# Attention scores over 96 rows, another opening, other norm chains and end, expert gates in pieces of 16 tokens and the fourth activation quarter in SBUF

## The chip, the cores and the metric

One core of a Trainium2 chip runs the whole program. Its engines are named as in the profile: PE (TensorE's matmuls; PEld its weight loads), DVE (VectorE), ACT (ScalarE), POOL (GpSimd), SP (SyncE, which here only issues DMAs). Times are microseconds on the device. The metric is the time of one execution; the kernel before took 1413.62 us, the median of three runs (1412.87 to 1416.95).

## The reference

256 tokens of 1024 channels, float32 throughout, go through two transformer blocks.

- First block: an RMS norm; projections; causal latent attention with 8 heads, whose queries and keys have 64 plain and 32 rotated channels (a score is a product over 96); causal differential attention with 4 heads of 2 x 64 channels; sigmoid gates on both branches; the output projection `wo` and residual; then norm, a gated FFN of 2816 hidden channels and residual; a final norm.
- Second block: modulation of the norms by `c` through `ada_w`; multiscale pooling and neighbourhood attention with context; `wo2` and residual; then, for each token, product-key top-k: 8 heads choose 16 of 128 x 128 = 16384 experts each. The output is `sum of gate * gelu(h . u_e) * v_e` over the chosen experts, plus residual and a last norm.

## The kernel before, in words

**Number format.** Nearly every matmul is done as three float32r products: `x_hi*w_hi`, `x_lo*w_hi`, `x_hi*w_lo` (`mm3`, lines 171 to 173). The weights come from DRAM in pieces of 128 x 2048 (`raw`, 1 MB, three buffers, issued on SP, line 154). For each block of 1024 columns ACT rounds them to `whi` (line 133) and DVE subtracts to `wlo` (line 130, `split`), into three buffers each. So PE has a steady stream as long as SP, ACT and DVE keep up; all three work through their own queue in order, PE too.

**Who sets the order.** The Tile framework plans the order of each engine's queue when the kernel is built, by a simulated timeline: what is ready by its estimate goes first, with the order of the program as priority, so that work of a later stage fills gaps of an earlier one. `tc.issue_after(ins)` keeps instructions on the same engine behind `ins`, and `tc.high_priority()` lifts some. `feed(n)` hands out the steps of a generator of side work (`side`) at n per pair of expert blocks.

**Stages, in order.**

1. *Opening.* SP loads `x` (transposed, 8 blocks of 128 channels) in two halves of 512 KB, the second between the first two weight pieces of 512 KB each (line 155). ACT and DVE split `x` into `xh` and `xl` (lines 343, 344). POOL squares `x` in two instructions (line 359), DVE adds the halves, PE sums over channels, and `rsqrt_cols` gives the norm: one DVE instruction for each column (line 216) and a power on POOL (line 219). Three small casts (lines 409 to 413) follow the first projection in the program.
2. *First attention.* Plain query channels are kept as `qn` (two heads to 128 rows), rotated ones as `qp` (four heads to 128 rows), and keys as `kn` and `kp`. `soft` (line 494) makes the scores of two heads: for each, a product over 64 rows and one over 32 rows into the same PSUM bank (line 501, full float32, two PE records each), and the mask (line 502). The value projection of the second attention (`lin_nat`, lines 202 to 204) and the gate projection need no scores and are planned between them.
3. *`wo`, FFN.* `put_x1` (line 611) adds the residual two blocks at a time and hands the squares to `SumSq`; `scaled_split` then makes the FFN's input `hs`. The FFN's first matmuls go ahead without the norm, which `hooks` bring in later. DVE also reduces `ada_w` here (`jk`, line 316).
4. *Second block up to the top-k queries.* Its norm after `wo2` (`ss3`, `put_x3`, line 816) is computed between the first matmuls of `wq` (line 840).
5. *Up pass.* `u_pass` runs four quarters of 32 expert blocks. A pair of blocks is 48 matmuls into one bank and a Gelu on ACT (line 1049). Quarters 0 and 1 stay in SBUF (`ga`), 2 and 3 go to DRAM through a ring (line 1051). The side work beside it is 44 steps of top-k and 33 steps of gates: for 8 tokens DVE makes one-hot tables, PE multiplies them, and ACT writes the dense gates of 128 x 128 experts to DRAM (`gg_d`, line 1015). It is fed at 1.2 steps a pair up to block 60, and at 1.7 from there; 8 steps were fed before.
6. *Second pass.* `v_pass` loads the gates of 16 expert blocks for all tokens (`gh`, 2 MB, line 1071, two buffers), multiplies them with the activations (line 1078), splits, and PE accumulates into four banks over all 128 expert blocks (line 1091). Quarters 2 and 3 come back from DRAM (`gr`, line 1076). The last two blocks are ordered by output bank, so that one bank after the other is done.
7. *End.* For both token halves: modulation, residual, square, norm and output (lines 1131 to 1141).

Of the kernel before, what the change touches and what calls it, by code (L numbers as in the profile page):

```python
# [20 lines left out]
P = 128  # L21
# [42 lines left out]
def block_kernel(ctx: ExitStack, tc: tile.TileContext, a: dict, out: bass.AP, dbg=None):  # L64
# [74 lines left out]
    class Weights:  # L139
# [68 lines left out]
    def rsqrt_cols(vs, scale, nm="n", eps=None):  # L208

        n = len(vs)  # L210
        y = small.tile([P, n], F32, tag=f"{nm}y{n}", name="ny")
        t = small.tile([P, n], F32, tag=f"{nm}t{n}", name="nt")
        for i, v in enumerate(vs):
            c = slice(i, i + 1)
            if eps is None:
                nc.vector.tensor_scalar(t[:, c], v, scale, EPS, op0=OP.mult, op1=OP.add)
            else:
                nc.vector.scalar_tensor_tensor(t[:, c], v, scale, eps, op0=OP.mult, op1=OP.add)
# [3 lines left out]
    class SumSq:  # L222
# [3 lines left out]
        def __init__(self, K, ps_fn, tail=2, held=False):  # L226
            self.held = [] if held else None
            self.K, self.k, self.ps, self.head = K, 0, [ps_fn() for _ in range(2)], K - tail
            self.first = True
# [3 lines left out]
        def add(self, src, scale=None, sq=None):  # L233
# [11 lines left out]
            if k >= self.head - 1:  # L245
                if self.held is None:
                    self.total(sq, k)
                else:
                    self.held.append((sq, k))

        def total(self, sq, k):
# [3 lines left out]
            self.first = False  # L255

        def done(self):
            for h in self.held or ():
                self.total(*h)
            return [p_[:, 0:1] for p_ in self.ps]  # L260
# [89 lines left out]
    subg = b1a.tile([P, 1], F32, name="subg")  # L350
    nc.scalar.activation(subg, col("sub"), AF.Copy, scale=1.0 - LAMBDA_INIT)
# [919 lines left out]
```

## Time and profile before

| | |
|---|---|
| median of three runs | 1413.62 us |
| the profiled execution's own time | 1420.62 us |
| its span, first to last instruction | 1418.8 us |
| mean granted clock of PE | 0.984 |
| chain that ended last, by engine | PE 88%, DVE 5%, DMA 4% |
| moved by DMA | 308.86 MB, mean 218 GB/s |

The profile is of one execution. The windows give, for a stretch, the busy time of each engine with the number of instructions (x), then the mean granted share of PE's clock (1.00 is 2.4 GHz, 0.50 is 1.2 GHz), the share of time in which the DMA engines were busy, and the rate. Matmuls are pipelined: the duration of one is longer than the step from one to the next, and a busy PE is not a PE at its peak. So PE is judged by how many matmuls it gets through in a stretch.

### The profile page before, as it was taken

How to read it: one execution, taken by the hardware profiler on the slowest of the kernel's cores; microseconds unless marked ns; L12 is line 12 of the kernel's file. 1: busy time of each engine (PE TensorE's matmuls, PEld its weight loads, DVE VectorE, ACT ScalarE, POOL GpSimd, SP SyncE). 2: the span in 40 equal slices, each digit the busy share in tenths (PEclk: the TensorE clock that was granted, in tenths of full speed). 3: DMA queues.
4: the chain of work that ended last, by engine and by line, in shares of the span. 5: the costliest groups of instructions: out<-in, count | busy, mean ns of one | idle time of the engine just before them, and what ended most of it. 6: DMA issues, size and time to landing. Idle time of an engine off the chain costs nothing.

```text
span 1418.8 us, 24208 instructions
## 1 busy us (share of the span) xinstructions
PE 1375.2 (97%) x9776; PEld 1270.8 (90%) x9776; DVE 1013.1 (71%) x1749; ACT 704.9 (50%) x1030; POOL 23.8 (2%) x25
## 2 busy tenths in 40 slices
PE   7999999999999999899999999998999999999997
PEld 6967998999999888899999999998888888888885
DVE  6774777998888646699984489876536555566775
ACT  4443654454546555545454456554344454444443
POOL 1000000000000001000000000000000000000000
PEclk9998999999999999999999999999899999999999
DMA  6452456777795632444555578889975555588762
GB/s 239 154 196 82 141 169 234 269 279 267 262 328 191 218 125 72 152 170 158 187 198 180 178 257 311 296 296 321 340 287 197 190 197 199 198 300 289 262 233 86
DMA packets 88448, 308.86 MB, mean 218 GB/s; under 512 B 6416, under 2 KB 39824, under 8 KB 61200
## 3 DMA queue, kind: packets, MB, share of 16 engines
q1 hardware_dynamic: 78544, 279.26, 57.0%
q10 hardware_dynamic: 9792, 28.05, 5.0%
q8 instruction: 76, 1.25, 0.3%
q14 instruction: 36, 0.29, 0.1%
HBM read 281.08 MB, written 26.21 MB: 217 GB/s over the span
## 4 chain that ended last, share of the span: by engine, by line
PE 88%; DVE 5%; DMA 4%; issue 1%; ACT 1%; POOL 0%; SPq 0%; ACTq 0%; POOLq 0%; DVEq 0%
PE acc L1091 24%; PE psa L173 9%; PE psa L171 9%; PE psa L172 9%; PE psc L173 8%; PE psc L171 8%; PE psc L172 8%; DMA aw<-in_ada 2%; PE psb L501 2%; DVE wlo L130 2%; PE psd L1012 1%; PE psb L1012 1%; DMA gh<-ggd 1%; PE psd L771 1%; PE psb L759 1%
## 5 line engine op out<-in xcount | busy, mean ns | idle before, releaser
L133 ACT ACTIVATE whi<-raw 128x1024 fp32r<-128x1024 f32 (+1 forms) x426 | 448.0, 1053 | 502.7 <-PE psa L172 181.6
L130 DVE TENSOR_TENSOR wlo<-raw,whi 128x1024 fp32r<-128x1024 f32 (+1 forms) x426 | 517.4, 1217 | 240.6 <-ACT whi L133 236.9
L171 PE MATMUL psc<-h2h,whi 128*128 128x256 f32 x1024 | 294.3, 288 | 6.4 <-ACT whi L133 6.4
L173 PE MATMUL psc<-h2h,wlo 128*128 128x256 f32 x1024 | 293.8, 288 | 4.2 <-DVE wlo L130 4.2
L172 PE MATMUL psc<-h2l,whi 128*128 128x256 f32 x1024 | 292.7, 286 | 0.0
L171 PEld LDWEIGHTS psc<-h2h,whi 128*128 128x128 f32 x1024 | 199.8, 195 | 7.0 <-ACT whi L133 7.0
L173 PEld LDWEIGHTS psc<-h2h,wlo 128*128 128x128 f32 x1024 | 199.5, 195 | 4.9 <-DVE wlo L130 4.9
L172 PEld LDWEIGHTS psc<-h2l,whi 128*128 128x128 f32 x1024 | 199.8, 195 | 0.0
L1091 PE MATMUL acc<-wlo,wgh 128*128 128x512 f32 x512 | 160.2, 393 | 0.0
L1091 PE MATMUL acc<-whi,wgl 128*128 128x512 f32 x512 | 158.7, 390 | 0.0
L1091 PE MATMUL acc<-whi,wgh 128*128 128x512 f32 x512 | 138.5, 389 | 0.0
L1091 PEld LDWEIGHTS acc<-whi,wgl 128*128 128x128 f32 x512 | 96.1, 188 | 20.2
L1091 PEld LDWEIGHTS acc<-whi,wgh 128*128 128x128 f32 x512 | 96.0, 188 | 20.1
L1091 PEld LDWEIGHTS acc<-wlo,wgh 128*128 128x128 f32 x512 | 94.6, 188 | 19.7
L171 PE MATMUL psa<-acth,whi 128*128 128x256 f32 x352 | 99.9, 284 | 2.0 <-DVE ft L638 1.2
L173 PE MATMUL psa<-acth,wlo 128*128 128x256 f32 x352 | 99.9, 284 | 1.9 <-DVE wlo L130 1.9
L172 PE MATMUL psa<-actl,whi 128*128 128x256 f32 x352 | 99.8, 284 | 0.2 <-DVE actl L293 0.2
L171 PE MATMUL psa<-xh,whi 128*128 128x256 f32 x240 | 71.1, 296 | 8.0 <-ACT whi L133 8.0
L173 PE MATMUL psa<-xh,wlo 128*128 128x256 f32 x240 | 70.4, 293 | 2.6 <-DVE wlo L130 2.6
L172 PE MATMUL psa<-xl,whi 128*128 128x256 f32 x240 | 71.0, 296 | 0.0
L316 DVE SCALAR_TENSOR_TENSOR jk<-aw,row_c 128x1024 bf16<-128x1024 f32 x48 | 58.6, 1220 | 14.8 <-DMA aw<-in_ada 14.4
L171 PEld LDWEIGHTS psa<-acth,whi 128*128 128x128 f32 x352 | 66.9, 190 | 2.6 <-ACT whi L133 1.4
(415 smaller groups left out, 2462.6 us busy)
## 6 DMA issues: line engine op xcount, KB each, us to landing
raw<-in_uT SPq DMA_DIRECT2D x64, 1024.0 KB, 4.9
raw<-in_v SPq DMA_DIRECT2D x64, 1024.0 KB, 4.9
aw<-in_ada SPq DMA_DIRECT2D x48, 512.0 KB, 5.8
raw<-in_wgu SPq DMA_DIRECT2D x22, 1024.0 KB, 4.9
ggd<-gs ACTq DMA_DIRECT2D x32, 512.0 KB, 4.5
gh<-ggd SPq DMA_DIRECT2D x8, 2048.0 KB, 14.3
raw<-in_wA SPq DMA_DIRECT2D x14, 1024.0 KB, 5.0
raw<-in_wdn SPq DMA_DIRECT2D x11, 1024.0 KB, 7.2
```

What stands on the lines that cost most here:

```text
L130: e.tensor_tensor(dst, src, hi.bitcast(F32), op=OP.subtract)
L133: nc.scalar.activation(dst_h, src, AF.Copy)
L171: nc.tensor.matmul(ps, wh, xs[0][:, k], start=(k == 0), stop=False)
L172: nc.tensor.matmul(ps, wh, xs[1][:, k], start=False, stop=False)
L173: last_mm[0] = nc.tensor.matmul(ps, wl, xs[0][:, k], start=False, stop=(k == K - 1))
L316: nc.vector.scalar_tensor_tensor(jk, aw, 1.0, c_, op0=OP.mult, op1=OP.mult, accum_out=dst[:, t:t + 1])
L501: nc.tensor.matmul(s[:, i], q_[:, qb * P:(qb + 1) * P], k_[:, :n], start=(j == 0), stop=False)
L759: nc.tensor.matmul(s, q2[x_][hd, hp, qs_], kall[y_][hd, hp], start=(i == 0), stop=(i == 2))
L771: nc.tensor.matmul(o[:, h * 64:(h + 1) * 64], pts[:, kb * P:(kb + 1) * P], v2[:, kb, h * 64:(h + 1) * 64], start=(kb == 0), stop=(kb == 3))
L1012: nc.tensor.matmul(ps[:, t4 * P:(t4 + 1) * P], o1[:, 2 * g4 + t4 // 2, :, t4 % 2], og[:, c, 2 * g4 + t4 // 2, :, t4 % 2], start=(c == 1), ...
L1091: r = nc.tensor.matmul(acc[tt][n], x_, w_[:, n * 512:(n + 1) * 512], start=st, stop=sp)
```

## The change

- Opening: `x` comes in four quarters issued on ACT's queue ahead of all else there; the first weights in pieces of 512, 512 and 1024 columns; ACT squares `x` instead of POOL; the casts move behind the last `put_in` of the first projection.
- Norm chains: `rsqrt_cols` takes all columns in one instruction; `SumSq` keeps one PSUM bank and runs its matmuls together when asked. `put_x1` and `put_x3` work block by block and make the next stage's split at once. `mdt` gets a pool of its own.
- Attention: queries and keys of a head stand as 96 rows in `qh` and `kh`, so that a score is one product. `nope` writes the two halves of a bank into two heads, the rope's last sum is written for four heads apart, and ACT copies `kp` into all eight heads.
- Experts: gates are stored in pieces of 16 tokens and read for 8 expert blocks (1 MB), issued behind the last weight load before them in the program. Quarter 3 stays in SBUF, in memory that the side work leaves; only quarter 2 goes to DRAM. The feed is 1.6 up to block 44, then 1.5; the ring has 3 buffers.
- End: the last three blocks are ordered by bank; the first token half is scaled on ACT; the second half's last bank skips one product.

```diff
-                    for o in range(0, w, 1024 if self.fine and c == 0 else w):
-                        e = o + (1024 if self.fine and c == 0 else w)
+                    ends = (0, 512, 1024, w) if self.fine and c == 0 else (0, w)
+                    for o, e in zip(ends, ends[1:]):
                         last_load[0] = nc.sync.dma_start(self.raw[:, o:e], self.src[:, c + o:c + e])
-                        if self.fine and c + o == 0:
-                            load_x(1)
...
-        for i, v in enumerate(vs):
-            c = slice(i, i + 1)
-            if eps is None:
-                nc.vector.tensor_scalar(t[:, c], v, scale, EPS, op0=OP.mult, op1=OP.add)
...
+        if eps is None:
+            nc.vector.tensor_scalar(t, v, scale, EPS, op0=OP.mult, op1=OP.add)
...
+        def done(self):
             for tt in range(2):
-                nc.tensor.matmul(self.ps[tt][:, 0:1], sq[:, tt * P:(tt + 1) * P], ones[:, 0:1],
-                                 start=self.first, stop=(k == self.K - 1))
...
+                for i, sq in enumerate(self.sqs):
+                    nc.tensor.matmul(self.ps[:, tt:tt + 1], sq[:, tt * P:(tt + 1) * P], ones[:, 0:1],
+                                     start=(i == 0), stop=(i == len(self.sqs) - 1))
+            return self.ps[:, 0:2]
...
-        k = slice(4 * i, 4 * i + 4)
-        nc.sync.dma_start(xT[:, k], a["xT"].rearrange("p (k t) -> p k t", k=KD)[:, k])
+        k = slice(2 * i, 2 * i + 2)
+        nc.scalar.dma_start(xT[:, k], a["xT"].rearrange("p (k t) -> p k t", k=KD)[:, k])
...
-        nc.gpsimd.tensor_tensor(sq0[:, k], xT[:, k], xT[:, k], op=OP.mult)
+        nc.scalar.activation(sq0[:, k], xT[:, k], AF.Square)
...
+                for r, o in outs(j, m):
+                    nc.vector.tensor_tensor(o, x_[r, j:j + m], t1[r, :m], op=OP.add)
...
+    nc.scalar.activation(kh[64:96], kp[64:96].to_broadcast([32, 8, S]), AF.Copy)
+
+    def nope(dst, j, n, ps, rb):
+        for e in range(2):
+            r = slice(64 * e, 64 * e + 64)
+            nc.vector.tensor_tensor(dst[0:64].rearrange("p (j e) t -> p e j t", e=2)[:, e, j:j + n], ps[r],
+                                    rb[r][:, None, :].to_broadcast([64, n, S]), op=OP.mult)
...
-            ptss = soft([[(qn[b0:b0 + 64, h // 2], kn[b0:b0 + 64, h // 2]),
-                          (qp[r0:r0 + 32, h // 4], kp[r0:r0 + 32, 0])] for h in pair], qb,
-                        [z[:, h:h + 1] for h in pair])
+            ptss = soft([[(qh[:, h], kh[:, h])] for h in pair], qb, [z[:, h:h + 1] for h in pair])
...
     def put_x1(j, n, ps):
-        nc.vector.tensor_tensor(x1[:, j:j + n], ps, xT[:, j:j + n], op=OP.add)
-        for i in range(n):
-            ss1.add(x1[:, j + i])
-
-    lin_t(a["wo"], 8, KD, (mh, ml), put_x1)
+        nc.vector.tensor_tensor(x1[:, j], ps[:, 0], xT[:, j], op=OP.add)
+        nc.scalar.activation(hs[0][:, j], x1[:, j], AF.Copy, scale=col("ffn", j))
+        nc.vector.scalar_tensor_tensor(hs[1][:, j], x1[:, j], col("ffn", j), hs[0][:, j].bitcast(F32),
+                                       op0=OP.mult, op1=OP.subtract)
+        ss1.add(x1[:, j])
+
+    lin_t(a["wo"], 8, KD, (mh, ml), put_x1, grp=1)
...
-    TG = 8
+    TG, TD = 8, 16
...
-                nc.scalar.dma_start(gg_d[:, i_], gs.rearrange("p j t -> p (j t)"))
+                if h + TG == TD:
+                    nc.scalar.dma_start(gg_d[:, i_ * TG // TD], gs.rearrange("p j t -> p (j t)"))
...
-            g = ga[q][:, j:j + 2] if q < 2 else ring.tile([P, 2, S], F32, tag="gr", name="gr")
+            g = ga[q][:, j:j + 2] if q != 2 else ring.tile([P, 2, S], F32, tag="gr", name="gr")
...
-            feed(1.2 if q * QJ + j < 60 else 1.7)
+            feed(1.6 if q * QJ + j < 44 else 1.5)
...
+    ga += [None, hot.tile([P, QJ, S], F32, bufs=1, name="ga3")]
+    u_pass(3)
...
-    HJ = 16
+    HJ = 8
...
-                gh = hot.tile([P, NG, HJ, TG], F32, tag="gh", name="gh")
-                nc.sync.dma_start(gh, gg_d.rearrange("p g (j t) -> p g j t", t=TG)[:, :, jj:jj + HJ])
+                gh = hot.tile([P, S // TD, HJ, TD], F32, tag="gh", name="gh")
+                with tc.issue_after(last_load[0].ins):
+                    nc.sync.dma_start(gh, gg_d.rearrange("p g (j t) -> p g j t", t=TD)[:, :, jj:jj + HJ])
...
-                        for i in range(2):
-                            r = block(i, tt, (n,))
+                        for b in range(NE - 3, NE):
+                            r = block(b, tt, (n,))
...
-            nc.vector.tensor_tensor(xn[:, h_], o[:, h_], fg[:, h_], op=OP.mult)
+            if tt == 0 or n == 0:
+                nc.vector.tensor_tensor(xn[:, h_], o[:, h_], fg[:, h_], op=OP.mult)
...
-        nc.vector.tensor_scalar(xn[:, hs_[1]], xn[:, hs_[1]], y, None, op0=OP.mult)
+        if tt == 0:
+            nc.scalar.activation(xn[:, hs_[1]], xn[:, hs_[1]], AF.Copy, scale=y)
+        else:
+            nc.vector.scalar_tensor_tensor(xn[:, hs_[1]], o[:, hs_[1]], y, fg[:, hs_[1]], op0=OP.mult, op1=OP.mult)
```

## Rows read from the trace of the kernel before

**Rows 1.** The page: busy time of each engine, share of the span, instructions.
```profile
PE 1375.2 (97%) x9776; PEld 1270.8 (90%) x9776; DVE 1013.1 (71%) x1749; ACT 704.9 (50%) x1030; POOL 23.8 (2%) x25
```

**Rows 2.** Windows: PE, PEld, DVE, ACT, POOL busy (x), clock, DMA share, GB/s.
```profile
743.00:820.00 77.00, 77.00 (x645) 77.00 (x644) 32.89 (x28) 34.75 (x43) 0.00 (x0) 1.00 0.55 189
...
960.00:1058.00 98.00, 87.40 (x653) 85.94 (x652) 52.93 (x62) 37.61 (x44) 0.00 (x0) 0.91 0.97 312
```

**Rows 3.** Waits over the span: who for whom, total us, times, longest us.
```profile
PE psa L173 <- DVE wlo L130: 6.2, 7, 2.6
...
PE psd L267 <- POOL ny L219: 1.7, 1, 1.7
...
DVE gr L1078 <- DMA gr<-gad: 20.6, 26, 3.0
```

**Rows 4.** Windows of two stretches of the first block, columns as above.
```profile
67.00:80.00 13.00, 13.00 (x62) 8.82 (x60) 12.37 (x18) 8.83 (x9) 0.00 (x0) 1.00 0.97 375
216.00:256.00 40.00, 35.94 (x290) 34.75 (x289) 32.94 (x51) 20.38 (x31) 1.61 (x1) 1.00 0.66 242
```

**Rows 5.** Windows inside the attention in which the clock is low.
```profile
82.20:85.50 3.30, 3.30 (x8) 2.02 (x8) 2.59 (x5) 0.81 (x4) 0.00 (x0) 0.50 0.00 0
...
106.10:116.20 10.10, 10.10 (x35) 7.16 (x34) 2.08 (x3) 2.02 (x6) 0.00 (x0) 0.50 0.00 0
```

**Rows 6.** SP's timeline around the end of the up pass: start, us, issue.
```profile
962.60 9.60 SPq L1071 DMA_DIRECT2D gh<-ggd  x2
...
1018.28 0.53 SPq L1071 DMA_DIRECT2D gh<-ggd  x1
1018.90 9.80 SPq L154 DMA_DIRECT2D raw<-in_uT  x3
```

**Rows 7.** DVE's timeline there, in brackets its idle time before and the releaser.
```profile
1008.54 4.90 DVE L1078 TENSOR_TENSOR ga<-ga,gh 128x512 f32<-128x512 f32 x8 [3.08 <-DMA gh<-ggd]
```

**Rows 8.** The chain that ended last, in three stretches: start, us, what.
```profile
79.59 0.83 PE psb L501 x4
...
1056.80 1.39 PE acc L1091 x6
...
1060.67 5.49 PE acc L1091 x24
```

**Rows 9.** The page's DMA issues: count, KB each, us to landing.
```profile
gh<-ggd SPq DMA_DIRECT2D x8, 2048.0 KB, 14.3
```

**Rows 10.** PE's timeline, scores of the second query block.
```profile
98.58 0.70 PE L501 MATMUL psb<-knope,qnope 64*128 64x256 f32 x2
99.21 0.69 PE L501 MATMUL psb<-kp,qp 32*128 32x256 f32 x2
```

**Rows 11.** Groups by form, 60 to 182 us: busy us, mean ns, idle before.
```profile
L477 DVE TENSOR_TENSOR qnope<-psa,rbq 128x512 f32<-128x512 f32 x2 | 1.4, 686 | 1.0 <-PE psa L173 1.0
```

**Rows 12.** The timeline of the opening, DVE and ACT.
```profile
6.25 4.50 DVE L344 SCALAR_TENSOR_TENSOR xl<-xT,cols,xh 128x256 fp32r<-128x256 f32 x4 [6.25 <-ACT xh L343]
...
11.88 1.66 DVE L344 SCALAR_TENSOR_TENSOR xl<-xT,cols,xh 128x256 fp32r<-128x256 f32 x4
...
16.33 2.00 ACT L133 ACTIVATE whi<-raw 128x1024 fp32r<-128x1024 f32 x2 [5.33 <-DMA raw<-in_wA]
```

**Rows 13.** DVE's timeline at the norm after `wo2`.
```profile
581.35 1.22 DVE L130 TENSOR_TENSOR wlo<-raw,whi 128x1024 fp32r<-128x1024 f32 x1
582.48 0.15 DVE L216 TENSOR_SCALAR nt<-psd 128x1 f32<-128x1 f32 x1
```

**Rows 14.** The timeline of the end: PE, DVE, ACT and POOL.
```profile
1408.97 0.39 PE L1091 MATMUL acc<-whi,wgl 128*128 128x512 f32 x1
...
1410.41 1.28 DVE L1132 TENSOR_TENSOR fin<-fin 128x512 f32<-128x512 f32 x2
...
1412.78 0.61 ACT L1133 ACTIVATE fin<-fin 128x512 f32<-128x512 f32 x1
...
1413.76 0.56 POOL L219 TENSOR_TENSOR ny<-nt,mhalf 128x1 f32<-128x1 f32 x1 [2.25 <-DVE nt L218]
```

More of the change, by code (lines that the diff above doesn't have):

```diff
@@ L222, in block_kernel, with __init__ @@
     class SumSq:
[L226 to L229, printed above, removed]
+        def __init__(self, K, ps_fn, tail=2):
+            self.K, self.k, self.ps, self.head = K, 0, ps_fn(), K - tail
+            self.sqs = []
             if self.head > 0:
@@ L350, in block_kernel @@
     subg = b1a.tile([P, 1], F32, name="subg")
+    for i in range(4):
+        load_x(i)
     nc.scalar.activation(subg, col("sub"), AF.Copy, scale=1.0 - LAMBDA_INIT)
-    load_x(0)
     split_x(0)
@@ L408, in block_kernel @@
     posf = b1s.tile([P, S], F32, name="posf")
-    nc.vector.tensor_copy(posf, posi)
     identb = b1a.tile([P, P], BF16, name="identb")
-    nc.vector.tensor_copy(identb, ident)
     maskb = b1a.tile([P, P], BF16, name="maskb")
-    nc.vector.tensor_copy(maskb, cs1[:, CB["mask"] - NCB])
+    with tc.issue_after(put[0].ins):
+        nc.vector.tensor_copy(posf, posi)
+        nc.vector.tensor_copy(identb, ident)
+        nc.vector.tensor_copy(maskb, cs1[:, CB["mask"] - NCB])
     def rope_tables(inv, nm):
@@ L437, in block_kernel, with rope @@
         s_d, c_d = rope_tables(col("inv1"), "d")
-    def rope(x_, n, rt, cc, ss):
+    def rope(x_, n, rt, cc, ss, outs=None):
         for j in range(0, n, 2):
@@ L571, in block_kernel @@
             nc.scalar.activation(t2[:, h], od[:, h], AF.Square, accum_out=ss[:, h:h + 1])
-        yd = rsqrt_cols([ss[:, h:h + 1] for h in range(4)], 1.0 / 128, "d")
+        yd = rsqrt_cols(ss, 1.0 / 128, "d")
         nc.vector.tensor_tensor(od, od, hb(yd, 4, P), op=OP.mult)
@@ L857, in block_kernel @@
     ga = [big.tile([P, QJ, S], F32, name=f"ga{q}") for q in range(2)]
-    ring = pool(ctx, "ring", 4)
+    ring = pool(ctx, "ring", 3)
     dram = ctx.enter_context(tc.tile_pool(name="dram", bufs=1, space=bass.MemoryType.DRAM))
-    ga_d = [dram.tile([P, QJ // 2, 2 * S], F32, name=f"gad{q}") for q in range(2)]
-    gg_d = dram.tile([P, NG, NE * TG], F32, name="ggd")
+    ga_d = dram.tile([P, QJ // 2, 2 * S], F32, name="gad")
+    gg_d = dram.tile([P, S // TD, NE * TD], F32, name="ggd")
     idxT = big.tile([P, 2, S], F16, name="idxT")
@@ L1082, in v_pass, with block @@
             end = jj + 2 == NE
-            hls = [w((j + i) * KD, KD) for i in range(2)]
-            def block(i, tt, ns):
-                hi, lo = hls[i]
-                first, last = jj + i == 0, jj + i == NE - 1
-                th, tl = wh[:, i, tt * P:(tt + 1) * P], wl[:, i, tt * P:(tt + 1) * P]
+            for i in range(2):
+                last3[jj + i] = *w((j + i) * KD, KD), wh[:, i], wl[:, i]
+            def block(b, tt, ns):
+                hi, lo, th, tl = last3[b]
+                first, last = b == 0, b == NE - 1
+                th, tl = th[:, tt * P:(tt + 1) * P], tl[:, tt * P:(tt + 1) * P]
                 for x_, w_, st, sp in ((th, hi, first, False), (th, lo, False, False), (tl, hi, False, last)):
@@ L1094, in v_pass @@
             if not end:
-                for i, tt in itertools.product(range(2), range(2)):
-                    block(i, tt, range(2))
+                for i, tt in itertools.product(range(1 if jj + 4 == NE else 2), range(2)):
+                    block(jj + i, tt, range(2))
             else:
@@ L1101, in v_pass @@
                     with tc.issue_after(r.ins) if r else nullcontext():
-                        for i in range(2):
-                            r = block(i, tt, (n,))
+                        for b in range(NE - 3, NE):
+                            r = block(b, tt, (n,))
     v_pass(0)
```

104 lines of the change are left out of this document (49 added, 55 removed).

## The prediction, before anything of the change was run

> **What bounds the kernel now.** I read the page first: PE is busy 97% of the span, no other engine over 71% [rows 1]. So a microsecond counts only if PE gets it. PE can lose time in three ways, and I read a view for each: it sits idle (the windows by stage, and the waits), it runs at the lower of its two clock levels (the windows that show the granted clock), or it executes matmuls that the change deletes (PE's timeline and the chain).
>
> The windows give the yardstick. From 743 to 820 us the up pass runs undisturbed: 645 matmuls in 77.0 us, 0.1194 us each. From 960 to 1058 us, the end of the up pass, 653 matmuls take 98.0 us [rows 2]; at the yardstick they would take 78.0. **20.0 us are lost there**, the largest loss in the trace. Smaller ones: a wait of 2.6 us among the first weights, 1.7 for one norm [rows 3], and from 216 to 256 us PE is idle for 4.1 of 40 us [rows 4]. The clock is at 1.2 GHz for 3.4 us from 82 and for 10.2 us from 106, inside the attention; half of that, 6.8 us, is lost [rows 5].
>
> **The parts and their costs.** The sum is made against the profiled execution, 1420.6 us (span 1418.8). The median of the runs shown is 1413.6, 7.0 lower; I take the same sum from it.
>
> **1, gates in pieces of 16 tokens and the fourth quarter in SBUF.** The 20.0 us: the side work is over by 960, the second pass may start early, and SP issues gh loads of 2 MB between the uT weight loads, six of them from 962 to 1019 [rows 6]. DMA then runs at a share of 0.97 [rows 2]. DVE sits 3.08 us on a gh load and then does eight gate products, 4.90 us, while the wlo that PE needs is queued behind them [rows 7]. PE starves, and its clock falls to a mean of 0.91 in that window [rows 2]. After the change a gh load is 1 MB, the first may be issued only after the last uT load, and the last quarter of the up pass writes nothing to DRAM. The last uT load is issued by 1028.7 [rows 6], PE's first acc matmul starts at 1056.8 [rows 8]; less the stalls in between, the first gh load has some 20 us, and one twice as large took 14.3 [rows 9]. Six loads cost 20.0, 3.3 each; I let one such cost remain: **-16.7**, bounds -10 (half of it is DVE running ahead with products, which the planner may do again) and -20.0. In the second pass a gh load stands on SP behind a weight load, and those run up to three buffers, three pairs of blocks, ahead. A pair takes 5.49 us there [rows 8], so a gh load leads its use by 16 to 22 us. I take nothing for it: DVE's waits on gr loads in that pass, 26 of up to 3.0 us, are none of PE's [rows 3]. What covers them are the three whi and wlo buffers; without them each would be a stall as in [rows 7].
>
> **2, heads of 96 rows.** For each of 8 heads and each of two query blocks one product (kp, qp) goes; the one over 96 rows has as many columns as the one over 64. Two products, four records, take 0.83 us in the first block [rows 8]; in the second each steps on by 0.63, the one over 64 rows as the one over 32 [rows 10]: 8 x 0.415 + 8 x 0.63 = **-8.4**. On DVE come four half-height writes of qh and kh and three more rope sums, 7 x 0.69 [rows 11] = 4.8 us, at a place (67 to 80 us) where DVE is busy 12.4 of 13.0 us. PE is busy 13.0 of 13.0 there [rows 4], and the planner fills its queue with the value and gate products, which need none of it: nothing; without that cover +4.8. ACT's broadcast of kp has 2048 columns, and ACT is idle for 4.2 of those 13.0 us: nothing.
> The Trainium skill ("TensorE: Matmul & The Clock Gate", Part 3) says that products on few rows in distinct row groups run at once; by it the deleted ones cost next to nothing and this term would be 0. The records above start one after the other, which speaks against it.
>
> **3, the clock in the attention.** The fall at 106 follows a stretch dense in 64- and 32-row products [rows 5, 10]. With half of those gone both falls may vanish (-6.8) or stay (0). No row decides, so I take half: **-3.4**.
>
> **4, the opening.** The squares leave POOL. While POOL squares, four xl on DVE take 4.50 us; right after it, four take 1.66 [rows 12]. So wlo can come 2.8 earlier, and PE's wait of 2.6 [rows 3] goes. The first pieces of x and of the weights are half as large, worth a few tenths more; but ACT sits until 16.33 for the weights of the third block [rows 12], and the same bytes are in front of them, so a gain here can be given back there. ACT does two squares over 1024 columns, about two of its whi, in the 5.33 us that it idles there: nothing. The casts that move behind the first put stand on DVE alone: nothing. **-2.8**, bounds 0 and -4.
> The Trainium skill ("DMA: Bandwidth & Descriptors", Issuing engines are not separate DMA queues) says that a second issuing engine saves only the time of issuing. By it x gains nothing from ACT's queue but its place in line; the sum takes nothing for the queue, so it stands.
>
> **5, norm chains.** rsqrt_cols becomes one instruction. Before, the planner put a wlo of 1.22 us between its two columns at 581 us [rows 13]; POOL, which PE waited 1.7 us for [rows 3], starts after the second: **-1.3**, bounds 0 and -1.7. At wo, blocks one by one cost DVE eight adds of 0.42 (as an xl [rows 12]) for four of 0.69, and one sum more: +1.0 on a DVE that is busy 32.9 of 40 and lets PE wait [rows 4]; the norm comes 1.2 earlier as above, and the splits of the last block sooner: **-1.0**, bounds +1.0 and -4.1.
>
> **6, feed rates.** 8 steps, then 22 x 1.6, then 22.5 x 1.5 make the 77 of the side work after 45 of 64 pairs, before the last quarter at 48, and the gate steps stand thinner than at 1.7: 0; if they were late, the rest would run before the last quarter with PE idle.
>
> **7, the end.** The last matmul ends at 1409.4; the last power on POOL starts at 1413.76, 4.4 later, behind DVE's products of both token halves [rows 14]. After: three blocks per group, nine matmuls at 5.49/24 [rows 8] = 2.1 us, against DVE's three steps of 0.64, so DVE is free when the last group ends. Then two steps of 0.64, a square of 0.61 with its sum, and the column: some 2.4 us. **-2.0**, bounds -1 and -2.6.
>
> Sum: -16.7 - 8.4 - 3.4 - 2.8 - 1.3 - 1.0 - 2.0 = -35.6. From 1413.6: **1378.0** (profiled: 1385.0).
>
> **Rivals.**
> (a) The collision stays by half, because gate products again stand ahead of wlo on DVE: part 1 gives 10, so 1384.7. For it: the products are as many as before. Against: one load, not six. 0.14.
> (b) Row groups overlap: parts 2 and 3 give nothing, 1389.8. Against: [rows 10]. 0.07.
> (c) The added DVE work reaches PE, and the opening stays bound by its bytes: +4.8 and +2.8, 1385.6. For it: DVE in [rows 4]. 0.12.
> (d) **Slower**: the 16 smaller loads come late in the second pass, and each of the 15 after the first costs PE what one of the six did, 3.3 us: +50, 1428. It decides from the point at which a 1 MB load takes longer than its lead of 16 to 22 us. For it: SP has twice as many such loads, bound to the weight loads' order. Against: 14.3 for 2 MB [rows 9]. 0.06; at ten of the boundaries 1411, no change: 0.04.
>
> **How the numbers follow.** The forecast has 0.57. A measurement of this kernel can tell 0.3%, 4.2 us. Faster by more than that: the forecast and (a) to (c), 0.90; within it 0.04; slower 0.06. The range: all strong bounds give -48.8, of which not all come, so I go to 1366; the weak one of part 1 with (b) or (c), and none for the clock, reaches 1398. Outside lie (d) and the far corners of the others, under 0.2.
>
> **What would show it.** The window before the first acc matmul at 0.12 us per matmul; no gh load among the uT loads; half as many records of MLA scores and fewer microseconds at 1.2 GHz in the attention; xl at 0.4 us each; POOL's last power 2.4 us after the last matmul. The prediction is wrong if PE waits for wlo behind gate products at many gh loads, or if the attention takes as long as before.

## The result, and the profile after

The changed kernel takes 1380.09 us, the median of four runs (1377.83 to 1383.19), against 1415.28 for the kernel before (four runs, 1412.87 to 1417.83): a ratio of 0.9753, with a 95% interval of 0.9723 to 0.9782. The forecast was 1378.0, range 1366 to 1398. The profiled execution took 1381.32 us (span 1379.1, mean granted clock 0.994); the forecast for it was 1385.0.

The page first: busy time of the engines [rows 1] and the gate loads among the DMA issues [rows 9].

```profile
PE 1349.9 (98%) x9736; PEld 1255.9 (91%) x9736; DVE 1013.3 (73%) x1746; ACT 708.1 (51%) x1034; POOL 20.0 (1%) x23
...
gh<-ggd SPq DMA_DIRECT2D x16, 1024.0 KB, 8.1
```

PE has 40 records fewer, 32 of them products of scores. A gate load lands after 8.1 us and not 14.3.

To see where the time went I cut both traces at the same points of the work: PE's first matmul on `kvh` (the attention starts), on `odh`, on `mh` (the merge), on `acth` (FFN), on `hidh` (the FFN's first half ends), on `cath` (`wo2`), on `h2h` (up pass) and into `acc` (second pass). The windows of the kernel before, for the attention, the FFN's first half and the up pass:

```profile
66.27:199.60 133.33, 133.33 (x865) 110.97 (x863) 88.14 (x132) 67.34 (x152) 2.93 (x2) 0.95 0.42 150
...
234.71:370.12 135.41, 131.34 (x1086) 130.16 (x1085) 119.73 (x187) 66.30 (x100) 3.15 (x2) 1.00 0.75 268
...
594.30:1056.64 462.34, 451.74 (x3943) 449.50 (x3944) 348.73 (x794) 229.11 (x299) 0.00 (x0) 0.98 0.69 239
```

And of the changed kernel: the last 98 us before the first `acc` matmul [rows 2], then attention, from `odh` to the merge, the FFN's first half, the stage of `wo2` and its norm, up pass and second pass.

```profile
921.00:1018.80 97.80, 97.80 (x813) 97.63 (x812) 45.16 (x40) 45.17 (x54) 0.00 (x0) 1.00 0.60 208
66.56:183.20 116.64, 115.24 (x831) 102.72 (x831) 90.55 (x132) 67.28 (x152) 2.02 (x2) 1.00 0.49 173
183.20:197.40 14.20, 13.36 (x96) 13.15 (x97) 9.23 (x12) 4.33 (x5) 0.00 (x0) 0.88 0.37 133
221.46:351.52 130.06, 129.38 (x1079) 128.97 (x1077) 117.65 (x180) 65.85 (x100) 1.78 (x1) 1.00 0.78 277
528.11:574.56 46.45, 39.71 (x312) 38.68 (x313) 31.04 (x55) 24.82 (x48) 1.79 (x1) 0.96 0.45 159
574.56:1017.73 443.17, 443.17 (x3943) 442.16 (x3944) 332.06 (x766) 228.00 (x299) 0.00 (x0) 1.00 0.60 216
1017.73:1371.32 353.59, 352.82 (x1570) 291.17 (x1568) 236.34 (x259) 171.12 (x200) 0.99 (x1) 1.00 0.70 237
```

The reader is to see three things. The end of the up pass holds 813 matmuls where it held 653 [rows 2], 0.1203 us each, at a DMA share of 0.60 and not 0.97. The attention is 16.7 us shorter, at a mean clock of 1.00 and not 0.95, and 1.4 us of idle PE have come into it; from `odh` to the merge it is 2.7 longer (11.52 before), at a clock of 0.88. And in the FFN's first half PE is idle for 0.7 us and not 4.1. SP's timeline shows why the up pass is smooth; a gate load is issued only behind the last uT load [rows 6]:

```profile
965.43 29.13 SPq L154 DMA_DIRECT2D raw<-in_uT  x6
994.65 0.84 SPq L1075 DMA_DIRECT2D gh<-ggd  x1
999.99 17.61 SPq L154 DMA_DIRECT2D raw<-in_v  x4
```

The waits that are left [rows 3]:

```profile
PE psa L169 <- DVE pq L885: 3.4, 1, 3.4
...
PE psd L255 <- POOL ny L215: 1.8, 1, 1.8
...
PE psa L169 <- ACT odh L580: 1.2, 1, 1.2
...
PE acc L1096 <- DVE wlo L130: 0.8, 1, 0.8
```

The longest wait for a wlo, 2.6 us in the opening, is gone. POOL's `ny` still keeps PE for 1.8 us, and two waits are new: `odh`, and a wlo just ahead of the last blocks of the second pass.

### The profile page after: what moved, and what is told of

Same layout as the page of the kernel before. It is cut to its first block, busy times and chain, and to the rows that moved or that the text cites. A ratio compares the mean times of both kernels' runs of the same rounds, so it can differ in the third digit from the quotient of the medians.

```text
span 1379.1 us, 24018 instructions
## 1 busy us (share of the span) xinstructions
PE 1349.9 (98%) x9736; PEld 1255.9 (91%) x9736; DVE 1013.3 (73%) x1746; ACT 708.1 (51%) x1034; POOL 20.0 (1%) x23
## 4 chain that ended last, share of the span: by engine, by line
PE 89%; DVE 5%; DMA 3%; issue 2%; ACT 1%; POOL 0%; SPq 0%; POOLq 0%; DVEq 0%; ACTq 0%
PE acc L1096 25%; PE psc L169 9%; PE psc L171 9%; PE psc L170 9%; PE psa L170 8%; PE psa L171 8%; PE psa L169 8%; DMA aw<-in_ada 3%; DVE wlo L130 2%; PE psd L1012 1%; PE psb L1012 1%; PE psd L774 1%; PE psb L505 1%; PE psb L762 1%; DVE jk L304 1%
## 5 line engine op out<-in xcount | busy, mean ns | idle before, releaser
L169 PE MATMUL psc<-h2h,whi 128*128 128x256 f32 x1024 | 290.9, 284 | 0.0
L171 PE MATMUL psc<-h2h,wlo 128*128 128x256 f32 x1024 | 289.8, 284 | 0.0
L170 PE MATMUL psc<-h2l,whi 128*128 128x256 f32 x1024 | 289.6, 283 | 0.0
L170 PEld LDWEIGHTS psc<-h2l,whi 128*128 128x128 f32 x1024 | 196.4, 192 | 0.0
L169 PEld LDWEIGHTS psc<-h2h,whi 128*128 128x128 f32 x1024 | 196.3, 192 | 0.0
L171 PEld LDWEIGHTS psc<-h2h,wlo 128*128 128x128 f32 x1024 | 196.1, 192 | 0.0
L1096 PE MATMUL acc<-whi,wgh 128*128 128x512 f32 x512 | 139.6, 390 | 0.0
L1096 PEld LDWEIGHTS acc<-wlo,wgh 128*128 128x128 f32 x512 | 95.1, 188 | 20.4 <-DVE wlo L130 1.1
L171 PEld LDWEIGHTS psa<-acth,wlo 128*128 128x128 f32 x352 | 67.6, 192 | 0.8 <-DVE wlo L130 0.8
```

Source lines behind the costliest of these rows:

```text
L169: nc.tensor.matmul(ps, wh, xs[0][:, k], start=(k == 0), stop=False)
L170: nc.tensor.matmul(ps, wh, xs[1][:, k], start=False, stop=False)
L171: last_mm[0] = nc.tensor.matmul(ps, wl, xs[0][:, k], start=False, stop=(k == K - 1))
L1096: r = nc.tensor.matmul(acc[tt][n], x_, w_[:, n * 512:(n + 1) * 512], start=st, stop=sp)
```

## The experiments

One table holds the stages of all kernels, in us from one profile each, cut at the points named above (opening: start to the first `kvh` matmul; FFN: its first half; tail: last matmul to the end of the span). The clock is the mean granted clock in the attention.

| kernel | opening | attention | clock | odh to merge | FFN | up pass | second pass | tail |
|---|---|---|---|---|---|---|---|---|
| before | 66.3 | 133.3 | 0.95 | 11.5 | 135.4 | 462.3 | 352.7 | 9.5 |
| 1 before, hold | 65.6 | 130.1 | 0.97 | 11.5 | 134.9 | 442.0 | 363.9 | 9.1 |
| 5 before, pieces | 65.8 | 139.6 | 0.90 | 11.5 | 135.3 | 446.3 | 352.5 | 9.7 |
| 6 before, both | 65.6 | 128.9 | 0.99 | 11.5 | 135.1 | 443.2 | 352.5 | 9.1 |
| 11 before, 96 rows | 66.8 | 116.4 | 1.00 | 14.1 | 133.0 | 458.7 | 352.7 | 10.1 |
| after | 66.6 | 116.6 | 1.00 | 14.2 | 130.1 | 443.2 | 353.6 | 7.8 |
| 2 no hold | 65.3 | 118.4 | 0.99 | 12.7 | 130.3 | 445.0 | 357.8 | 7.8 |
| 3 quarter in DRAM | 65.5 | 116.4 | 1.00 | 12.7 | 130.1 | 443.0 | 353.6 | 7.8 |
| 4 pieces of 8 tokens | 63.7 | 116.6 | 1.00 | 14.1 | 130.1 | 442.9 | 353.4 | 7.8 |
| 7 two products | 63.7 | 141.4 | 0.89 | 11.5 | 131.6 | 444.0 | 353.6 | 7.8 |
| 8 old `wo` boundary | 65.0 | 116.9 | 1.00 | 14.2 | 133.9 | 442.9 | 353.6 | 7.8 |
| 9 POOL, columns | 67.1 | 116.9 | 1.00 | 14.2 | 130.7 | 443.1 | 353.6 | 7.8 |
| 10 order | 66.9 | 116.2 | 1.00 | 12.7 | 133.9 | 443.3 | 353.6 | 7.8 |
| 12 two blocks | 63.6 | 116.7 | 1.00 | 14.2 | 130.1 | 443.0 | 352.5 | 11.3 |

Before and after differ in the profiled spans by 39.7 us: opening +0.3, attention -16.7, odh to merge +2.7, merge to FFN +0.5, FFN -5.4, the modulation and context stages +0.2, `wo2` and its norm -1.3, up pass -19.2, second pass +0.9, tail -1.7.

Two of these can't be read from one pair of profiles. From `cath` to `h2h` (`wo2` and its norm) the four profiles before, 1, 5 and 6 take 46.2 to 47.8 us, mean 46.7, and the seven with the changed kernel's code there (after, 2 to 4, 7, 8, 12) 45.0 to 48.1, mean 46.9: the -1.3 is chance. And the opening of one and the same code takes 63.6 to 66.6 us. PE's part of the windows from 6.40 to 18.50 us, of the changed kernel and of run 12, which have the same opening:

```profile
6.40:18.50 12.10, 11.07 (x45) 1.00 0.98 379
```

```profile
6.40:18.50 12.10, 11.24 (x71) 1.00 1.00 384
```

PE steps at 0.21 us per matmul first and at 0.12 later, though the granted clock of the window is 1.00 in both; in the changed kernel's profile it steps faster from 18.5 us on, in run 12 from 12.5.

### The gates: hold, pieces, quarter

**1. The hold alone, on the kernel before.**

```diff
+                with tc.issue_after(last_load[0].ins):
                     nc.sync.dma_start(gh, gg_d.rearrange("p g (j t) -> p g j t", t=TG)[:, :, jj:jj + HJ])
```

> The kernel before with one line changed: a gate load (gh, still 2 MB, 16 expert blocks) is issued only behind the last weight load ahead of it in the program, so none goes out among the uT loads. All else is the kernel before, the fourth quarter still in DRAM. Theory (the loss of 20.0 us at the end of the up pass is the gh loads' collision with the uT loads and the products that DVE then does ahead of wlo): 16 to 20 us faster, 1395 to 1399 against 1415, and the last 653 matmuls of the up pass at 0.12 us each. Rival A (the bytes do it: the fourth quarter's activations written beside the uT loads): 0 to 4 us faster, 1411 to 1415. Rival B (the first 2 MB load, which took 14.3 us, is then late for the first product): half, 1404 to 1408, with PE waiting once between the two passes.

Measured: 1405.84 us, ratio 0.9937 (0.9917 to 0.9956). By the cut at the first `acc` matmul the up pass is 20.4 us shorter and the second pass 11.2 longer. Here 22 matmuls of the up pass come after that cut (3920 records against 3943), 22 x 0.12 = 2.6 us; with them the up pass is 17.7 us shorter, of the 20.0 that the prediction had counted as lost, and the second pass 8.5 longer. The windows of the two passes, and DVE's timeline in the second, with its idle time in brackets:

```profile
587.81:1029.78 441.97, 440.56 (x3920) 439.35 (x3921) 332.71 (x769) 228.30 (x299) 0.00 (x0) 1.00 0.63 224
1029.78:1393.66 363.88, 357.45 (x1592) 294.82 (x1590) 232.96 (x254) 172.07 (x200) 0.00 (x0) 1.00 0.72 245
```

```profile
1069.62 4.91 DVE L1079 TENSOR_TENSOR ga<-ga,gh 128x512 f32<-128x512 f32 x8 [2.84 <-DMA gh<-ggd]
```

This is [rows 7] over again, moved into the second pass: 2.84 us for the load, then eight products, 4.91 us, ahead of wlo. PE waits three times in the second pass, 2.83, 1.40 and 2.20 us. So the total is that of rival B, but not by one wait between the passes.

**5. The pieces alone, on the kernel before** (16 tokens, 8 expert blocks a load).

```diff
-    TG = 8
+    TG, TD = 8, 16
...
-    HJ = 16
+    HJ = 8
```

> The kernel before with gates in pieces of 16 tokens and gate loads of 8 expert blocks, 1 MB, twice as many; no hold, the fourth quarter in DRAM, the feed as before. Theory (a load is paid for by what DVE does behind it: a wait for it and all its products, four now and not eight, 2.5 us, which the three whi and wlo buffers cover): most of the 20.0 us at the end of the up pass comes back without any hold, 12 to 18 us faster, 1397 to 1403 against 1415, and the second pass as long as before. Rival A (among the uT loads any gate load collides, whatever its size; only the hold helps): within 4 us of 1415. Rival B (half the size, half the loss): 1405.

Measured: 1401.52 us, ratio 0.9891 (0.9861 to 0.9921). The up pass is 16.0 us shorter though gate loads still stand among the uT loads, and the second pass is as before; in the up pass PE waits twice, for wlo, 1.61 and 0.63 us, where it waited six times before, three times for whi and three for wlo.

**6. Pieces and hold together, on the kernel before.**

> The kernel before with both: pieces of 16 tokens with loads of 8 expert blocks, and the hold behind the weight loads; the fourth quarter still goes to DRAM. Theory: the up pass as with the hold alone (442 us from the first wq products after the norm to the first acc matmul, against 462 before), and the second pass as before (353 us, against 364 with the hold and 2 MB loads): 19 to 21 us faster, 1394 to 1397. Rival (the quarter in SBUF is needed for the rest): 1398 to 1406.

Measured: 1395.42 us, ratio 0.9869 (0.9839 to 0.9899). Up pass 19.2 us shorter, second pass 0.3 shorter: all of what the changed kernel has there, without its quarter in SBUF.

**2. The changed kernel without the hold** (the edit of 1 taken back).

> The changed kernel without the line that holds gh loads behind the weight loads; pieces of 16 tokens, 1 MB loads and the fourth quarter in SBUF stay. Theory (the hold carries the gain): gh loads stand among the uT loads again, and 8 to 20 us are lost at the end of the up pass, 1388 to 1400 against 1380. Rival A (the quarter in SBUF carries it): within 4 us of 1380. Rival B (two loads of 1 MB are half of what two of 2 MB were, so half of the loss): 1390.

Measured: 1385.49 us, ratio 0.9775 (0.9756 to 0.9794), which overlaps with the changed kernel's 0.9753. The profile tells more: 1.8 us more in the up pass and 4.2 in the second, where PE waits 2.52 us for a wlo behind this:

```profile
1270.47 2.50 DVE L1081 TENSOR_TENSOR ga<-ga,gh 128x512 f32<-128x512 f32 x4 [2.32 <-DMA gh<-ggd]
```

So the hold does not carry the gain by itself. What has to be short is the time for which DVE is away from wlo: its wait for the load and the products of that load. Eight products behind a late load cost PE up to 2.8 us a time; four cost it 2.52 here, but at one load only of this pass.

**3. The fourth quarter through DRAM.**

```diff
-            if q == 2:
-                nc.scalar.dma_start(ga_d[:, j // 2], g.rearrange("p j t -> p (j t)"))
+            if q >= 2:
+                nc.scalar.dma_start(ga_d[q - 2][:, j // 2], g.rearrange("p j t -> p (j t)"))
```

> The changed kernel with the fourth quarter of the activations written to DRAM and read back as before (ring of four buffers); hold, pieces of 16 tokens and 1 MB loads stay. Theory (the hold carries the gain, 4 MB out and 4 MB back find room): within 4 us of 1380. Rival A (the quarter in SBUF carries it): 10 to 20 us slower, 1390 to 1400, lost at the end of the up pass. Rival B: the loads of the quarter come late in the second pass, 16 waits of 0.3 to 0.6 us there, 1385 to 1390, the up pass unchanged.

Measured: 1379.64 us, ratio 0.9744 (0.9727 to 0.976), up pass and second pass the same to 0.2 us. The quarter in SBUF brings nothing by itself.

**4. Gates in pieces of 8 tokens, loads still of 1 MB.**

```diff
-    TG, TD = 8, 16
+    TG, TD = 8, 8
```

> The changed kernel with gates in pieces of 8 tokens as before, while a load is still of 8 expert blocks and 1 MB, so that its contiguous runs halve (8 blocks x 8 tokens against 8 x 16) and their number doubles. Theory (a gh load leads its use by 16 to 22 us, so that even one that takes as long as the 2 MB load before, 14.3 us, is hidden): within 4 us of 1380, the load's landing time up from 8.1 to 10 to 16 us. Rival (d) of the prediction (small gh loads come late in the second pass): up to 3.3 us for each of 15 loads, up to 1430, with PE waits between pairs there.

Measured: 1378.68 us, ratio 0.9745 (0.9725 to 0.9765). A gate load lands after 9.4 us and not 8.1, less than the 10 to 16 expected, and no PE wait comes with it. Rival (d) had its point where a load takes longer than its lead of 16 to 22 us; halved runs do not reach it, so past that point it is untested. Of "16 tokens and 8 blocks" it is the 8 blocks that count.

### The attention

**7. Two products again, on the same tiles.**

```diff
-            ptss = soft([[(qh[:, h], kh[:, h])] for h in pair], qb, [z[:, h:h + 1] for h in pair])
+            ptss = soft([[(qh[0:64, h], kh[0:64, h]), (qh[64:96, h], kh[64:96, h])] for h in pair], qb, [z[:, h:h + 1] for h in pair])
```

> The changed kernel with each score of the first attention as two products again, one over the 64 plain rows and one over the 32 rotated rows of the same 96-row tiles; DVE and ACT do what they do in the changed kernel. Theory (each product steps on by its own time): 8 x 0.415 + 8 x 0.63 = 8.4 us slower, 1388.5. Rival A (products of 64 and of 32 rows in other row groups run at once): within 2 us of 1380. Rival B (the scores' products lie beside waits that the changed kernel has at the end of the attention, 1.2 and 0.8 us for odh and odl, and these go): 6.3 us slower, 1386.5.

Measured: 1401.3 us, ratio 0.9904 (0.9876 to 0.9932): 21 us slower than the changed kernel, more than any theory had. The windows of the whole attention and of one stretch in it:

```profile
63.67:205.05 141.38, 141.38 (x862) 117.27 (x863) 91.08 (x131) 67.55 (x151) 2.02 (x2) 0.89 0.40 142
...
106.00:133.20 27.20, 27.20 (x95) 19.66 (x95) 9.14 (x15) 6.88 (x21) 0.00 (x0) 0.50 0.03 13
```

PE is busy for all of the 141.38 us, and for 27.2 of them in one piece it has 1.2 GHz and not 2.4. A mean of 0.89 over 141.38 us is 15.6 us lost; what is left is 125.8. So the second product costs 125.8 - 116.6 = 9.2 us, and the clock the rest. In the changed kernel's 116.6 PE is idle for 1.4; of PE's own steps it is 125.8 - 115.2 = 10.6. From `odh` to the merge it is 2.7 us shorter: the waits for `odh` and `odl` are gone, as rival B had it.

The prediction's price of 8.4 is for the deleted products alone. The one that is left got quicker too. PE in the changed kernel, at the full clock:

```profile
98.55 0.65 PE L505 MATMUL psb<-kh,qh 96*128 96x256 f32 x2
99.03 0.22 PE L506 MATMUL psb<-maskb,identb 128*128 128x128 bf16 x1
99.09 0.65 PE L505 MATMUL psb<-kh,qh 96*128 96x256 f32 x2
```

The product over 96 rows steps on after 0.48 us; over 64 rows it took 0.63, and over 32 as well [rows 10]. By the starts of all records at the full clock, one record (half a product) over 96 rows takes 0.23 us at 256 columns and 0.13 at 128, in the changed kernel as in runs 3 and 11, and one over 64 or 32 rows 0.31 and 0.21, in the kernel before as in run 7. An estimate from these for the 16 scores: 8 x (1.26 - 0.47) + 8 x (0.83 - 0.26) = 10.9 us. Why fewer rows take longer was not tried.

**11. The 96 rows alone, on the kernel before** (`qh`, `kh`, `nope` and the one product; `ki`, `kf` single and `mdt` in its own pool, for room).

> The kernel before with the heads as 96 rows alone (qh, kh, one product per score; the buffers ki and kf single and mdt in a pool of its own, which make room for the tiles); opening, norms, experts and end as before. Theory (the product that goes costs its step, and with it go most of the stretches at 1.2 GHz): from the first product of the kv projections to the first of odh 116 to 119 us, against 126 to 140 in the profiles of kernels with two products (116.6 to 118.4 with one), and no more than 3.4 us at 1.2 GHz in it; PE then waits about 2 us for odh and odl, which it did not before. In all 10 to 16 us faster, 1400 to 1405. Rival (the clock in the attention was kept up by another part, the opening or the FFN boundary): 6 to 9 us faster, 1407 to 1409, with 10 us and more at 1.2 GHz.

Measured: 1397.98 us, ratio 0.985 (0.9821 to 0.9879).

```profile
66.79:183.23 116.44, 115.32 (x830) 102.74 (x830) 90.91 (x138) 67.40 (x153) 2.01 (x2) 1.00 0.50 174
```

The attention is that of the changed kernel, with its clock and its waits (0.92 and 0.84 us for `odh` and `odl`). So both come with the 96 rows (and what makes room for them), and with no other part. The total is lower than expected: the norm after `wo2` came out 3.9 us shorter than before and the unchanged up pass 3.6; 2.4 of the first is PE's wait for `pq`, 2.8 us before and 0.4 here. What did it, the pool or another order, was not tried.

### The boundary, the norms, the opening, the end

**8. The boundary from `wo` to the FFN as before.**

```diff
-        nc.vector.tensor_tensor(x1[:, j], ps[:, 0], xT[:, j], op=OP.add)
-        nc.scalar.activation(hs[0][:, j], x1[:, j], AF.Copy, scale=col("ffn", j))
...
+        nc.vector.tensor_tensor(x1[:, j:j + n], ps, xT[:, j:j + n], op=OP.add)
...
+    hs = scaled_split(x1, KD, lambda k: col("ffn", k), acts, "act")
```

> The changed kernel with the boundary from wo to the FFN as before: the residual two blocks at a time, the squares, and only then the split of the FFN's input by itself. Theory (as predicted, small): 1.0 us slower. Rival A (the two traces: from the FFN's first matmul to its last hidden block 130.1 us against 135.2 before, PE idle 0.6 us against 3.7 in the first 22 us): 4 to 5 us slower, 1384 to 1385, with the waits for acth and wlo back. Rival B (those waits went by other parts, the sums in one bank or the pool of mdt): within 1 us.

Measured: 1383.65 us, ratio 0.978 (0.9753 to 0.9806). The FFN takes 3.8 us more, and PE's waits are back, among them this one:

```profile
220.20:354.06 133.86, 130.70 (x1083) 129.65 (x1081) 119.07 (x186) 66.48 (x100) 3.15 (x2) 1.00 0.75 270
```

```profile
PE psa L169 <- DVE ft L640: 1.3, 1, 1.3
```

The order that the planner finds has a part in it: in run 10, which leaves this boundary as changed, the same stretch takes 133.9 us as well, with one wait of 2.1 us for `ft`.

**9. Two small parts undone: POOL's squares, and one multiply-add for each column.**

```diff
-        nc.scalar.activation(sq0[:, k], xT[:, k], AF.Square)
+        nc.gpsimd.tensor_tensor(sq0[:, k], xT[:, k], xT[:, k], op=OP.mult)
...
-            nc.vector.tensor_scalar(t, v, scale, EPS, op0=OP.mult, op1=OP.add)
...
+        for i in range(n):
+            c = slice(i, i + 1)
...
+                nc.vector.tensor_scalar(t[:, c], v[:, c], scale, EPS, op0=OP.mult, op1=OP.add)
```

> The changed kernel with two small parts undone, far apart in time and read from the profile each by itself: the squares of x on POOL again, and the norms' multiply-add one instruction for each column again. Theory, opening (POOL's squares slow what DVE does beside them): the eight xl take 1.0 to 1.2 us each in pairs of 0.4 now, PE's waits before 13 us grow by up to 2.6 us. Rival, opening (x comes in quarters now, so the squares fall behind the xl): waits as now, within 0.3 us. Theory, norm after wo2 (the power on POOL lasts as long as the DVE instruction beside it, a wlo, so it ends at the same time whichever way): PE's wait for ny within 0.2 us of 1.78. Rival (as the prediction had it): one column more puts the power off, and the wait grows by 0.2 to 1.3 us. In all 1380 to 1385.

Measured: 1382.64 us, ratio 0.977 (0.9745 to 0.9795), so the sum can't be told from the changed kernel's. DVE's timeline of the opening:

```profile
6.51 2.07 DVE L130 TENSOR_TENSOR wlo<-raw,whi 128x512 fp32r<-128x512 f32 x1 [0.41 <-ACT whi L133]
...
9.90 2.50 DVE L334 SCALAR_TENSOR_TENSOR xl<-xT,cols,xh 128x256 fp32r<-128x256 f32 x2
```

Beside POOL's squares a wlo takes 2.07 us and two xl 2.50; in the changed kernel 0.69 and 0.88. PE waits 1.31, 0.47 and 0.52 us there, against 0.32 and 0.67: the squares on ACT are worth 1.3 us of waiting. At the norm PE's wait for `ny` is 1.78 us, as with one instruction.

**10. Two changes of order, on the changed kernel.**

```diff
+        with tc.issue_after(xh_last[0].ins):
             nc.scalar.activation(sq0[:, k], xT[:, k], AF.Square)
...
         y4 = rsqrt_cols(ss3.done(), 1.0 / D)
+        yc4 = small.tile([P, 2], F32, name="yc4")
+        wq.hold = nc.vector.tensor_copy(yc4, y4)
...
+                    with tc.issue_after(self.hold.ins) if self.hold and self.at >= 2 else nullcontext():
                         split(hi[:, o:o + step], lo[:, o:o + step], r[:, o:o + step], lo_eng.next())
```

> The changed kernel with two changes of order: ACT squares x behind the last xh, and at the norm after wo2 a DVE copy that reads the power's result is put behind the multiply-add, with the third and fourth wlo of wq held behind the copy, so that DVE does nothing while POOL works. Theory, opening: the waits of 0.3 and 0.7 us for xh and xl at 11 to 13 us go, 1.0 us. Theory, norm: the power lasts 0.7 and not 1.79 us, and PE's wait for it falls from 1.78 to about 0.8 us. In all 2 us faster, 1378. Rival (the power's 1.79 us are POOL's own): it lasts 1.7 to 1.8 us again, the two wlo come that much later, and PE waits 1 us longer for them: 1380 to 1381.

Measured: 1377.96 us, ratio 0.973 (0.9711 to 0.9749), which overlaps with the changed kernel's. The question was POOL's power at the norm. In the changed kernel, DVE and POOL [rows 13]:

```profile
561.06 0.16 DVE L212 TENSOR_SCALAR nt<-psd 128x2 f32<-128x2 f32 x1 [3.62 <-PE psd L246]
561.30 2.36 DVE L130 TENSOR_TENSOR wlo<-raw,whi 128x1024 fp32r<-128x1024 f32 x2
...
561.30 1.79 POOL L215 TENSOR_TENSOR ny<-nt,mhalf 128x2 f32<-128x2 f32 x1 [40.46 <-DVE nt L212]
```

And in this kernel, where DVE holds still:

```profile
562.13 0.71 POOL L216 TENSOR_TENSOR ny<-nt,mhalf 128x2 f32<-128x2 f32 x1 [39.74 <-DVE nt L213]
...
562.87 0.17 DVE L844 COPY yc<-ny 128x2 f32<-128x2 f32 x1 [0.82 <-POOL ny L216]
562.95 2.35 DVE L130 TENSOR_TENSOR wlo<-raw,whi 128x1024 fp32r<-128x1024 f32 x2
```

The same power takes 1.79 us beside a wlo and 0.71 alone, and PE's wait for it is gone. But the wait that follows, for `pq`, grows from 3.4 to 5.3 us, so the two together are 5.3 us against 5.2. From the first `cath` to the first `h2h` matmul it is 45.4 us against 46.5, which lies within the 45.0 to 48.1 of the changed kernel's code: no gain is shown. In the opening the wait of 0.32 is still 0.24 and that of 0.67 stays.

**12. The last two blocks by bank, not the last three.**

```diff
-                        for b in range(NE - 3, NE):
+                        for b in range(NE - 2, NE):
```

> The changed kernel with the last two expert blocks ordered by bank, as before, and not the last three; the other parts of the end stay. Theory: PE's wait of 0.77 us for a wlo, which stands before the last 36 matmuls in each profile of the changed kernel and in none before, goes; DVE is still at the bank before when the last group ends, so the time from the last matmul to the end grows from 7.8 by 0 to 0.6 us. In all within 1 us of 1380. Rival (the wait is there with two blocks too, and DVE is late): up to 1 us slower.

Measured: 1383.28 us, ratio 0.9751 (0.9729 to 0.9772), no difference that the totals show. The profile: the second pass is 1.1 us shorter, the wait of 0.77 is gone, and the tail is 3.5 longer, where the theory had 0 to 0.6.

```profile
1368.48 1.29 DVE L1137 TENSOR_TENSOR fin<-fin 128x512 f32<-128x512 f32 x2
...
1368.65 2.13 POOL L215 TENSOR_TENSOR ny<-nt,mhalf 128x1 f32<-128x1 f32 x1 [808.19 <-DVE nt L214]
...
1370.82 0.72 ACT L1144 ACTIVATE fin<-fin,ny 128x512 f32<-128x512 f32 x1 [3.41 <-POOL ny L215]
```

The power of the first token half lasts 2.13 us beside DVE's products without a gap, ACT's scaling waits for it, and the squares of the second half stand behind that scaling.

## Why the prediction held, term by term

The sum came out at 35.2 by the medians against the predicted 35.6, by terms that err both ways, and that it came so near is in part luck. Between the two profiles, where the stages can be read, it is 39.7: the attention gave 4.9 more than its two terms and the `wo` boundary 4.4 more, the opening 3.1 less, and 2.7 were lost between `odh` and the merge, for which there was no term. Two sums of the range are off: the strong bounds add up to -47.6, not -48.8, and the weak corner to 1395.7 with (c) and 1396.5 with (b), not 1398.

1. **The gates, -16.7.** Right in place and mechanism: the up pass gave 19.2, its last stretch runs at 0.1203 us per matmul, no gate load stands among the uT loads. The step that failed is "I let one such cost remain": none did. And the one cost left of six was counted for the hold; run 5 shows that the halved products do 16 of it without any hold, and run 1 that the hold without them gives 8.5 us back in the second pass. What I took at nothing, the second pass, cost 0.1 beyond the wait of 0.77 that comes from the end's three blocks. The quarter in SBUF is worth nothing (run 3).
2. **The 96 rows, -8.4.** 9.2 us by run 7; by the table, without the clock's loss, 133.3 x 0.95 = 126.7 before and 116.6 after, 10.1. The products do step one after the other, and what is over 8.4 has its reason in the step "the one over 96 rows has as many columns as the one over 64", which took the two for equally long: the one over 96 rows is the quicker, 0.47 against 0.63 us at 256 columns, so that PE's steps fall by 10.6 (run 7), of which 1.4 come back as waits. The Trainium skill ("TensorE: Matmul & The Clock Gate", Part 3) has products on distinct row groups run at once, each with an output slice of its own. Here the two add into the same one, and in the kernel before half of the heads have plain and rotated rows in one row group, so its case is not tested, and no overlap shows: runs 7 and 11 have 9.2 and 10.3 us (126.7 - 116.4) where rival (b) has 0. DVE's added work did not reach PE, as said. Not seen: PE, with 9 us less to do, now waits for `odh` and `odl`, 1.2 and 0.8 us (not in run 7, but in run 11), and in six of the nine profiles with one product the clock falls behind that wait (0.88 in the window above). That costs 1.2 to 2.7 us.
3. **The clock, -3.4.** The direction was right, the size half. In the five profiles with two products the attention's mean clock was 0.95, 0.97, 0.90, 0.99 and 0.89; over their spans (133.3, 130.1, 139.6, 128.9, 141.4 us) that is 6.7, 3.9, 14.0, 1.3 and 15.6 us lost, 8.3 on average. In the nine with one product it was 0.99 once and 1.00 in the others. So in this pair of profiles the strong bound, 6.8, came and not the middle; how much it is in a given execution is luck.
4. **The opening, -2.8.** PE's idle time up to the first `kvh` did shrink by 2.6 us, but the stage took 66.6 us against 66.3. PE started 1.5 us earlier and stepped at 0.21 us per matmul until 18.5 us; before, until 17.3. That is this execution and not the change: in the six other profiles with the same opening the first steps of 0.12 come at 10.0 to 12.8 us, also in run 2, where PE waits for xh and xl as it does here (0.54 and 0.87 us), and in the three of them where the step does not fall back to 0.21 for some 3 us afterwards (4, 7 and 12) the stage takes 63.6 to 63.7. Over profiles with the same opening code the stage varies, 65.6 to 66.8 in the five old ones (mean 66.0) and 63.6 to 66.6 in the seven new ones of runs 2 to 4, 7, 8, 12 and after (mean 64.8): the term is about 1.2 on average, near 0 in the profile shown.
5. **The norms.** `wo2`, -1.3: nothing came. The wait for `ny` went from 1.7 to 1.8, and is 1.78 with one instruction for each column too (run 9). What stood between the columns, a wlo, now stands beside the power and holds it (run 10). That the stage lost 1.3 in this pair of profiles is its clock, 0.93 before and 0.96 after, and luck: its mean is 46.7 over the profiles with the old code there and 46.9 with the new. The Trainium skill ("SBUF — State Buffer", Who interferes with whom) says that a DVE instruction with two inputs from SBUF and a POOL instruction that reads SBUF keep each other out. By it the term would have been near 0; the trace agrees, with 0.71 against 1.79 and 2.13 us. [rows 12] had shown it for the opening, and I did not carry it to the norms. `wo` and FFN, -1.0: 3.8 by run 8, near the strong bound of 4.1; the weak end, DVE's added adds, did not come. How much of it is the boundary and how much the order that the planner finds is open (run 10).
6. **The end, -2.0.** The tail gave 1.7: the last power starts at 1374.02, 2.7 us after the last matmul, where 2.4 was forecast. ACT's scaling of the first half stands ahead of the second half's squares. A wait of 0.77 us for a wlo came with the three blocks.

Of the rivals, (a) and (d) fell with runs 2 and 4 to 6, (b) with 7 and 11, and of (c) one half came: DVE's added work reached no PE, but the opening gave less than half of its term.

## What to carry to other kernels

A load that feeds a burst of work on an engine which others wait for is best sized by that burst: the engine is away for the wait and for all products of one load, and only what its buffers cover is free. Holding such loads back moved a part of the collision here (17.7 us gained, 8.5 given back); halving them removed most of it (16.0 of 19.2).

Where two engines share a way to memory, removing an instruction between two dependent steps can leave the second one slowed by what moves up beside it: read the duration of the short instruction in both places before counting the gap as won. And an end of one engine's work that is brought forward shows at the next wait (here from `ny` to `pq`), so a saving is taken from what all waits up to there add up to, not from the one that went. Nor is the length of a stage from one profile enough: at the same code it moved by 3 us in the opening and at `wo2`.

## What was not expected of the hardware

PE without a gap can still lose its clock: in run 7 it was busy for 27.2 of 27.2 us at a granted 0.50, in a stretch that mixes score products over 64 and 32 rows and small transposes with 33 products of a projection. How long that lasts differs from one profile to the next of the same code (a mean clock of 0.90 to 0.99 in the attention of kernels whose attention is that of before), and the executions of the kernel before go with their clock: of the seven beside run 11 the shortest took 1410.56 us at a mean clock of 0.990, one of the longest 1420.57 at 0.980. Merging the 64 and 32 rows into 96 took nearly all of it away.

A float32 product over 96 rows steps on faster than one over 64 or 32 rows, 0.47 against 0.63 us at 256 columns.

A power over 128 x 2 numbers on POOL takes 0.71 us while DVE is idle, 1.79 beside one wlo, and over 128 x 1 it takes 2.13 beside three DVE products in a row.
